# Head outputs of an mLSTM encoder turned by VectorE in 32x32 blocks instead of by TensorE, with the gates and the branch's DRAM copies laid out to match

## The chip, the cores and the metric

The kernel runs on one core of a Trainium2 chip. The metric is the device time of one execution in microseconds (us). The profile comes from one further execution, recorded by the hardware profiler.

## What is computed

One encoder layer over 1024 prompt tokens and 256 sample tokens with 1024 channels, all in float32. Cut to what matters here:

```python
h = rms_norm(x, norm_g) * (1.0 + scale) + shift          # scale, shift, gate from c @ w_ada
cb, cc, cx, cz, q, k, v, o, mz, gpre, gmerge = split(h @ w_in)
y_conv = cb * centred_dwconv3(cc * cx, conv_w, conv_b) * silu(cz)
h_fwd = mlstm_chunkwise(q, k, v, gates)                  # 4 heads of 256, chunks of 128 tokens
h_bwd = flip(mlstm_chunkwise(flip(q), flip(k), flip(v), flipped gates))
hm = h_fwd + h_bwd
hm = hm * rsqrt(mean(hm * hm, per head) + EPS) * mh_norm_g
y_m = sigmoid(o) * hm * silu(mz)
merged = sigmoid(g1) * (y_conv @ w_proj_conv) + sigmoid(g2) * (y_m @ w_proj_mlstm)
out = rms_norm(x + gate * (merged @ w_out), final_norm_g)
```

## The kernel before

Tokens of both sequences stand side by side, T = 1280, in ten chunks of 128 (eight and two). Large products are made of float32 operands split into a high and a low part (fp32r), three matmuls a product.

**Input projection** (to about 1180 us). Channels stand on partitions, tokens in the free dimension in two halves of 640. Strassen pairs (class Strassen; matmuls at L755, weight splits at L329 on ACT and L330 on POOL, evictions at L672) make in this order gate columns, head 0, og_pair, conv_pairs and the other heads. og_pair combines sigmoid(o) and silu(mz) into one gate (up to constant factors) and stores it by L797 and L802 as [channel, token] in og_dr, one DMA of 320 KB for a block of 128 channels and half of the tokens. by_tokens (L878) turns k and v by VectorE in blocks of 32x32 (L881) and stores each with four DMAs whose pieces are 32 floats long.

**Sweeps** (about 1180 to 1467 us). For each head one sweep over the chunks in one direction keeps its results in "kept", then a second one in the other direction runs while the next head's first does. Sweep.query (L1341) multiplies queries with the state C, Sweep.state (L1359) makes the state's update, which VectorE adds (L1365, L1367). Class Pairs finishes the second sweep two chunks at a time: scores (L1402), values (L1439 to L1460), and finish: RMS factor per token, scaled on ACT (L1482), then four transposes on TensorE (L1489) into two PSUM tiles "misc", a multiplication with the norm's weight mhq and the gate og on VectorE (L1492, reads PSUM, writes og), and two stores to ym_dr [channel, token] (L1499). Class Filler gives TensorE units of the convolution projection in between (L1581 to L1583); PACE says how many units are recorded by which step s.

**After the sweeps.** first_ym loads the second half of the tokens of ym_dr through the three "th" buffers, which the filler units use too, and splits it into high (L1602, ACT) and low (L1603, VectorE); it is called for heads 0 and 1 at step 45, for heads 2 and 3 behind the last step. merge runs the mLSTM projection (proj_y, L1514 to L1516; accumulators in eight PSUM banks that the sweeps' tiles held before), finish the output projection (L1726 to L1728). The first half's y is loaded by load_y (L1680 to L1682) meanwhile.

**What sets the order.** Up to the end of the sweeps the operations of all engines, SP's DMA issues among them, are recorded on a Board. It plays them as a list schedule by durations given by hand: what can start first goes first, within 0.25 us the lower step, and operations marked low last. Buffers of a tag go out in the order of their recording. All DMAs but a few small ones at the start are issued by SP, in that order, and each engine works through its queue in order. Behind the sweeps a scheduler orders the rest and may put its DMAs further ahead.

## Time and profile before

| | us |
|---|---|
| median of 3 runs (lowest, highest) | 1707.37 (1704.66, 1707.56) |
| the profiled execution | 1706.05 |
| its span, first to last instruction | 1704.3 |
| TensorE busy | 1657.9 (97%) |
| VectorE, ACT, POOL busy | 996.0, 579.4, 677.9 |
| DMA traffic | 241.87 MB, mean 142 GB/s |

Busy time counts any instruction on the engine. Matmuls are pipelined, so the distance between their starts, not their length, is what one costs. The granted clock was 0.993 on average. PE is TensorE, PEld its weight loads, DVE is VectorE, SPq the queue of SyncE that issues DMAs.

### The profile page before, as it was taken

Reading aid. Unit: us, or ns where it says so; the run is one execution under the profiler, and the core shown is the slowest. Engines: PE = TensorE matmul, PEld = TensorE weight load, DVE = VectorE, ACT = ScalarE, POOL = GpSimd, SP = SyncE. Lnnn points to the kernel's source line nnn. Section 1 sums busy time; section 2 is a strip of 40 time slices with the busy share of each in tenths; the row PEclk is TensorE's granted clock in tenths of the full one; section 3 lists DMA queues with packets and bytes.
Section 4 is the critical chain, followed back from the end, with each engine's and each line's share of the span. In section 5 each row is a group of like instructions: output and inputs, shape, how many; then the busy total and the mean of one; then the engine's idle time right before and its main releaser. Section 6 shows DMA issues by size and latency. Waiting matters only on the chain.

```text
span 1704.3 us, 27694 instructions
## 1 busy us (share of the span) xinstructions
PE 1657.9 (97%) x10542; PEld 1571.2 (92%) x10542; DVE 996.0 (58%) x1689; ACT 579.4 (34%) x1121; POOL 677.9 (40%) x499
## 2 busy tenths in 40 slices
PE   7889999999999999999999999999999999999997
PEld 1789999899999999999999999999988889898985
DVE  1795434456555655666666886652257777565645
ACT  2753232123544222222222222122256565333322
POOL 1124333234655576676667643333210101223412
PEclk9899999999999999999999999999999999999999
DMA  8224325323554122212222565558778855783631
GB/s 331 93 92 142 120 92 137 61 83 103 151 151 126 53 69 81 81 57 65 66 69 69 146 143 132 130 126 266 264 249 278 270 181 162 230 283 121 236 109 62
DMA packets 280536, 241.87 MB, mean 142 GB/s; under 512 B 96100, under 2 KB 237652, under 8 KB 280404
## 3 DMA queue, kind: packets, MB, share of 16 engines
q1 hardware_dynamic: 280224, 240.06, 46.1%
q8 instruction: 84, 1.38, 0.3%
q14 instruction: 48, 0.39, 0.1%
q10 hardware_dynamic: 180, 0.04, 0.0%
HBM read 171.16 MB, written 68.89 MB: 141 GB/s over the span
## 4 chain that ended last, share of the span: by engine, by line
PE 91%; DVE 4%; issue 1%; DMA 1%; ACT 1%; ACTq 0%; SPq 0%; POOL 0%; DVEq 0%; POOLq 0%
PE acc L755 61%; PE qc L1341 3%; PE u L1359 3%; PE accd L1515 2%; PE accd L1514 2%; PE accd L1516 2%; PE accd L1727 2%; PE accd L1728 2%; PE accd L1726 2%; PE acc L1582 2%; PE acc L1581 2%; PE acc L1583 2%; PE acc L480 2%; PE misc L1402 1%; PE misc L1442 1%
## 5 line engine op out<-in xcount | busy, mean ns | idle before, releaser
L330 POOL TENSOR_TENSOR wl<-comb,wh 128x512 fp32r<-128x512 f32 x176 | 248.2, 1411 | 290.2 <-ACT wh L329 277.8
L672 DVE TENSOR_TENSOR q<-acc,q 128x640 f32<-128x640 f32 x272 | 220.8, 819 | 217.5 <-PE acc L755 215.0
L330 POOL TENSOR_TENSOR wl<-raw,wh 128x512 fp32r<-128x512 f32 x136 | 190.0, 1398 | 243.8 <-ACT wh L329 240.7
L755 PE MATMUL acc<-xt,wh 128*128 128x320 f32 x1408 | 264.3, 310 | 0.0
L755 PEld LDWEIGHTS acc<-xt,wh 128*128 128x128 f32 x1408 | 220.8, 188 | 0.4
L329 ACT CAST wh<-comb 128x512 fp32r<-128x512 f32 x176 | 108.8, 619 | 285.4 <-PE acc L755 276.9
L329 ACT CAST wh<-raw 128x512 fp32r<-128x512 f32 x136 | 84.3, 621 | 281.9 <-PE acc L755 215.3
L755 PE MATMUL acc<-xt,wl 128*128 128x320 f32 x704 | 160.6, 310 | 0.0
L1542 POOL TENSOR_TENSOR wl<-raw,wh 128x512 fp32r<-128x512 f32 x28 | 36.3, 1299 | 232.2 <-ACT wh L1541 232.2
L755 PEld LDWEIGHTS acc<-xt,wl 128*128 128x128 f32 x704 | 117.7, 188 | 0.0
L628 DVE TENSOR_TENSOR comb<-raw 128x512 f32<-128x512 f32 x88 | 72.8, 827 | 47.3 <-DMA raw<-in_w_in_dram 31.0
L822 POOL TENSOR_TENSOR big<-big,q 128x640 f32<-128x640 f32 x48 | 78.6, 1638 | 36.9 <-DVE q L672 28.5
L572 ACT ACTIVATE q<-q,zero 128x640 f32<-128x640 f32 x76 | 63.2, 831 | 85.7 <-DVE q L672 78.6
L628 DVE TENSOR_TENSOR comb<-raw,comb 128x512 f32<-128x512 f32 x44 | 45.9, 1043 | 66.0 <-POOL wl L330 66.0
L755 PE MATMUL acc<-b11H,wh 128*128 128x320 f32 x352 | 81.4, 312 | 2.8 <-ACT wh L329 2.8
L755 PE MATMUL acc<-t2L,wh 128*128 128x320 f32 x352 | 80.2, 309 | 2.1 <-DVE t2L L384 2.1
L1514 PE MATMUL accd<-y,wh 128*128 128x320 f32 x256 | 79.6, 311 | 2.7 <-DVE og L1492 1.5
L755 PE MATMUL acc<-b00H,wh 128*128 128x320 f32 x352 | 81.9, 313 | 0.0
L755 PE MATMUL acc<-b10H,wh 128*128 128x320 f32 x352 | 80.7, 310 | 0.4 <-DVE q L672 0.4
L755 PE MATMUL acc<-t2H,wh 128*128 128x320 f32 x352 | 80.6, 310 | 0.4 <-ACT t2H L383 0.4
L755 PE MATMUL acc<-b11H,wl 128*128 128x320 f32 x352 | 80.5, 309 | 0.4 <-POOL wl L330 0.4
L755 PE MATMUL acc<-b11L,wh 128*128 128x320 f32 x352 | 80.6, 310 | 0.0
(318 smaller groups left out, 4151.1 us busy)
## 6 DMA issues: line engine op xcount, KB each, us to landing
raw<-in_w_in_dram SPq DMA_DIRECT2D x96, 256.0 KB
raw<-in_w_in_dram SPq DMA_DIRECT2D x46, 512.0 KB
th<-th_dr SPq DMA_DIRECT2D x32, 320.0 KB
th_dr<-q SPq DMA_DIRECT2D x28, 320.0 KB
raw<-in_w_proj_conv_dram SPq DMA_DIRECT2D x16, 512.0 KB
k<-kn_dr SPq DMA_DIRECT2D x64, 128.0 KB
raw<-in_w_proj_mlstm_dram SPq DMA_DIRECT2D x16, 512.0 KB
raw<-in_w_out_dram SPq DMA_DIRECT2D x16, 512.0 KB
```

Of the source, the lines that this page charges most:

```text
L329: op("ACT", .63, lambda: A.copy(wh[:], src()), r=r, w=[wh])
L330: op("POOL", 1.4, lambda: G.tensor_tensor(out=wl[:], in0=src(), in1=fp(wh[:]), op=ALU.subtract), r=[*r, wh], w=[wl])
L480: op("PE", .88, lambda h=h, j=j, kt=kt, wa=wa: PE.matmul(pada[h][0:4, j, :], cz4()[:, kt, :], wa()[:, j * 512:(j + 1) * 512], start=kt == ...
L572: A.activation(out, in_, AF.Tanh, bias=zero[:, 0:1], scale=0.5)
L628: op("DVE", .9, lambda: V.tensor_tensor(out=t[:], in0=x(), in1=y(), op=o), r=[x.tok, y.tok], w=[t])
L672: op("DVE", .82, lambda: V.tensor_tensor(out=two(dst()), in0=acc[:, :, 0:TQ], in1=two(t()), op=ALU.add), r=[acc, t.tok], w=[dst.tok])
L755: PE.matmul(acc[:, q, 0:TQ], st_[:, k_, :], m_[:, q * TQ:(q + 1) * TQ], start=k_ == 0 and n == 0, stop=k_ == 3 and n == 2)
L822: op("POOL", 1.65, lambda: G.tensor_tensor(out=dst(), in0=dst(), in1=t(), op=ALU.mult), r=[dst.tok, t.tok], w=[dst.tok])
L1341: PE.matmul(pq[:, 0:HD + 2], qTs[i][:, kd, c * P:(c + 1) * P], C[:, kd, :], start=kd == 0, stop=kd == 1)
L1359: PE.matmul(pu[:, db, 0:HD + 2], k[:, db * P:(db + 1) * P], wv[:], start=True, stop=True)
L1514: PE.matmul(accs[q][:, :TQ], wh, yH, start=kt == 0, stop=False)
L1542: op("POOL", 1.36, lambda wh=wh, wl=wl, src=src: G.tensor_tensor(out=wl[:], in0=src(), in1=fp(wh[:]), op=ALU.subtract), r=[raw, wh], w=[wl])
```

## The change

The head outputs of a pair are turned by one VectorE transpose, from SBUF to SBUF, in square blocks of 32x32 that stay in their place in the grid of blocks, and multiplied with the gate in a second VectorE operation. The gate is stored by og_pair in the matching order: og_dr is now [head, block of 32 tokens, channel in its block, block of channels, token in its block]; each of its 16 stores becomes four. The result goes to ym_dr, now [head, chunk, channel, token], by four DMAs for each pair in place of two, with pieces of 32 floats. The loads of ym_dr (first_ym, load_y) read it chunk by chunk, five pieces of 128 floats a channel in place of one of 640. The norm's weight mhq is left out of the sweeps' multiplication and applied where the loaded values are split: ACT's copy becomes a copy with scale, VectorE's subtraction a multiply and subtract. load_y does this a block of 128 channels at a time. Two more edits stand with it: PACE after step 21, and first_ym for heads 2 and 3 at step 50.

```diff
-    ym_dr = dram.tile([D, T], F32, name="ym_dr")
-    og_dr = dram.tile([D, T], F32, name="og_dr")
+    ym_dr = dram.tile([NH, NC, HD, P], F32, name="ym_dr")
+    og_dr = dram.tile([NH, T // 32, 32, HD // 32, 32], F32, name="og_dr")
...
+    def store_og(n, l, t):
+        for b in range(4):
+            store(80, og_dr[n // 2, l * 20:(l + 1) * 20, :, n % 2 * 4 + b, :].rearrange("x i j -> i x j"),
+                  lambda b=b: t()[32 * b:32 * b + 32].rearrange("p (x j) -> p x j", j=32), [t.tok])
...
-            store(320, og_dr[n * P:(n + 1) * P, lo_], to["o"], [to["o"].tok])
+            store_og(n, 0, to["o"])
...
-            store(320, og_dr[n * P:(n + 1) * P, hi_], t, [t.tok])
+            store_og(n, 1, t)
...
-            load(256, lambda: self.og[:], og_dr[h * HD:(h + 1) * HD, g * P:(g + 2) * P].rearrange("(b p) t -> p b t", p=P),
-                 (), [(self.og, 0), (self.og, 1)])
+            load(256, lambda: self.og[:], og_dr[h, 4 * g:4 * g + 8].rearrange("(c a) i b j -> (a i) c (b j)", a=4), (), [self.og])
...
-            for db in range(2):
-                py = buf(psB, [P, 512], F32, "misc", 3)
-
-                def turn(db=db, py=py):
-                    for j in range(2):
-                        PE.transpose(py[:, j * P:(j + 1) * P], qcf[:, j, db * P:(db + 1) * P], ident[:])
-
-                def gated(db=db, py=py):
-                    V.scalar_tensor_tensor(out=og[:, db, :], in0=py[:, :2 * P],
-                                           scalar=mhq[:, 2 * h + db:2 * h + db + 1], in1=og[:, db, :],
-                                           op0=ALU.mult, op1=ALU.mult)
-
-                r0 = h * HD + db * P
-                op("PE", .3, turn, r=[(qcf, 0), (qcf, 1)], w=[py])
-                op("DVE", .48, gated, r=[py, (og, db)], w=[(og, db)])
-                op("SP", 128, lambda db=db, r0=r0: dma(ym_dr[r0:r0 + P, g * P:(g + 2) * P], og[:, db, :]),
-                   r=[(og, db)], w=[("ym", h, g, db)])
+
+            z = buf(mp_, [P, 2, HD], F32, "z", 2)
+            op("DVE", .72, lambda: V.transpose(z[:], qcf[:, :, :HD]), r=[(qcf, 0), (qcf, 1)], w=[z])
+            op("DVE", .65, lambda: V.tensor_tensor(out=z[:], in0=z[:], in1=og[:], op=ALU.mult), r=[z, og], w=[z])
+            for a in range(4):
+                op("SP", 64, lambda a=a: dma(
+                    ym_dr[h, g:g + 2, :, 32 * a:32 * a + 32].rearrange("c (b i) j -> i (c b) j", i=32),
+                    z[32 * a:32 * a + 32].rearrange("p c (b j) -> p (c b) j", j=32)), r=[z], w=[("ym", h, g, a)])
...
+    def scaled_h(out, x, kt):
+        A.activation(out, x, AF.Copy, bias=0.0, scale=mhq[:, kt:kt + 1])
+
+    def scaled_l(out, x, hi, kt):
+        V.scalar_tensor_tensor(out=out, in0=x, scalar=mhq[:, kt:kt + 1], in1=fp(hi), op0=ALU.mult, op1=ALU.subtract)
...
-    PACE = [min(4 + s, 12) if s < 10 else 12 + (s - 9) * 4 // 7 if s < 17 else 16 if s < 21 else min(17 + (s - 21) * 13 // 28, 30) if s < 50 else 32
+    PACE = [min(4 + s, 12) if s < 10 else 12 + (s - 9) * 4 // 7 if s < 17 else 16 if s < 21 else min(16 + (s - 21) // 2, 32)
...
-        if s == 45:
-            ym0 = [first_ym(0)]
-    ym0.append(first_ym(1))
+        if s in (45, 50):
+            ym0.append(first_ym(s // 48))
...
-                dma(raw[:], v[:, 4 * n + k:4 * n + k + 2, t0:t0 + TH2])
-                A.copy(yH[:, k:k + 2], raw[:])
-                V.tensor_tensor(out=yL[:, k:k + 2], in0=raw[:], in1=fp(yH[:, k:k + 2]), op=ALU.subtract)
+                for j in range(2):
+                    dma(raw[:, j].rearrange("p (c t) -> p c t", t=P), ym_rows(4 * n + k + j, c0))
+                    scaled_h(yH[:, k + j], raw[:, j], 4 * n + k + j)
+                    scaled_l(yL[:, k + j], raw[:, j], yH[:, k + j], 4 * n + k + j)
```

## Rows read from the trace of the kernel before

**Rows 1.** The page: busy time of the engines; the chain that ended last.

```profile
PE 1657.9 (97%) x10542; PEld 1571.2 (92%) x10542; DVE 996.0 (58%) x1689; ACT 579.4 (34%) x1121; POOL 677.9 (40%) x499
...
PE 91%; DVE 4%; issue 1%; DMA 1%; ACT 1%; ACTq 0%; SPq 0%; POOL 0%; DVEq 0%; POOLq 0%
```

**Rows 2.** Stretches: busy us of PE, PEld, DVE, ACT, POOL; clock, DMA share, GB/s.

```profile
400.00:700.00 300.00, 300.00 (x2048) 300.00 (x2047) 175.47 (x183) 109.82 (x213) 180.28 (x125) 1.00 0.36 104
...
1265.00:1300.00 35.00, 34.44 (x192) 30.24 (x190) 24.54 (x84) 21.29 (x57) 3.81 (x3) 1.00 0.77 249
1300.00:1350.00 50.00, 48.93 (x276) 43.06 (x275) 37.50 (x132) 30.66 (x85) 2.56 (x2) 1.00 0.87 285
1350.00:1400.00 50.00, 50.00 (x283) 44.93 (x283) 37.89 (x135) 31.53 (x87) 3.82 (x3) 1.00 0.66 211
1400.00:1440.00 40.00, 39.55 (x245) 36.56 (x244) 31.52 (x114) 23.03 (x63) 6.49 (x5) 1.00 0.51 157
1440.00:1468.00 28.00, 26.21 (x174) 24.94 (x174) 19.65 (x59) 14.79 (x38) 8.17 (x6) 1.00 0.59 185
```

**Rows 3.** Timeline of PE, one pair's four turns: start us, us, what.

```profile
1435.41 0.60 PE L1489 MATMUL misc<-ident,qcf 128*128 128x128 f32 x4
1435.85 0.61 PE L1402 MATMUL misc<-kT,qT 128*128 128x128 f32 x4
```

**Rows 4.** Groups by line: shapes xcount | busy us, mean ns | idle before.

```profile
L1489 PE MATMUL misc<-ident,qcf 128*128 128x128 f32 x80 | 12.5, 275 | 0.3 <-ACT qcf L1482 0.2
...
L1492 DVE SCALAR_TENSOR_TENSOR og<-misc,mhq,og 128x256 f32<-128x256 f32 x40 | 17.5, 477 | 5.7 <-PE misc L1489 5.7
...
L881 DVE STREAM_TRANSPOSE q<-q 128x640 f32<-128x640 f32 x32 | 27.0, 845 | 1.1
```

**Rows 5.** Timeline of PE where the sweeps end.

```profile
1463.99 0.31 PE L1583 MATMUL acc<-b10H,wl 128*128 128x320 f32 x1
1464.48 0.95 PE L1489 MATMUL misc<-ident,qcf 128*128 128x128 f32 x4 [0.18 <-ACT qcf L1482]
1466.89 0.41 PE L1514 MATMUL accd<-y,wh 128*128 128x320 f32 x1 [1.46 <-DVE og L1492]
...
1470.52 0.31 PE L1514 MATMUL accd<-y,wh 128*128 128x320 f32 x1
1472.04 0.41 PE L1514 MATMUL accd<-y,wh 128*128 128x320 f32 x1 [1.20 <-ACT y L1602]
```

**Rows 6.** Timelines of DVE, SP and PE from there on.

```profile
1464.74 1.31 DVE L1603 TENSOR_TENSOR y<-th,y 128x640 fp32r<-128x640 f32 x1
1465.97 0.86 DVE L1492 SCALAR_TENSOR_TENSOR og<-misc,mhq,og 128x256 f32<-128x256 f32 x2
1466.42 0.38 SPq L318 DMA_DIRECT2D th<-ym_dr  x1
1472.02 0.83 DVE L1603 TENSOR_TENSOR y<-th,y 128x640 fp32r<-128x640 f32 x1 [3.38 <-ACT y L1602]
1549.71 1.49 DVE L1682 TENSOR_TENSOR y<-yraw,y 128x1280 fp32r<-128x1280 f32 x1 [1.76 <-ACT y L1681]
1575.84 0.40 PE L1728 MATMUL accd<-wh,mL 128*128 128x512 f32 x1
```

**Rows 7.** DMA issues by tile, ns min/median/max; then one stretch as in Rows 2.

```profile
L321 SPq DMA_DIRECT2D v_dr<-q x64: 302/508/1986, 303.3 to 1158.2; - x64
L321 SPq DMA_DIRECT2D og_dr<-q x16: 320/333/343, 386.3 to 560.6; - x16
L1499 SPq DMA_DIRECT2D ym_dr<-og x40: 319/378/1026, 1268.9 to 1467.4; - x40
...
1125.00:1126.00 1.00, 1.00 (x7) 0.94 (x7) 0.96 (x2) 0.01 (x1) 0.91 (x1) 1.00 0.97 144
```

**Rows 8.** Tile k: its loads and readers, ns min/median/max, first and last start.

```profile
L318 SPq DMA_DIRECT2D k<-kn_dr x64: 319/320/1750, 1182.4 to 1402.1; - x64
L1359 PE MATMUL u<-wv,k x256: 378/381/486, 1188.4 to 1430.5; 128*128 128x258 f32 x128
```

More of the change, by code (lines that the diff above doesn't have):

```diff
@@ L1592, in unit, with ym_rows @@
                 op("SP", 320, lambda: dma(zc_dr[n * P:(n + 1) * P, t0:t0 + TH2], th[:]), r=[(th, 0), (th, 1)], w=[("zc", n, b)])
+    def ym_rows(kt, c0):
+        return ym_dr[kt // 2, c0:c0 + 5, kt % 2 * P:(kt % 2 + 1) * P, :].rearrange("c p t -> p c t")
+    def scaled_h(out, x, kt):
+        A.activation(out, x, AF.Copy, bias=0.0, scale=mhq[:, kt:kt + 1])
+    def scaled_l(out, x, hi, kt):
+        V.scalar_tensor_tensor(out=out, in0=x, scalar=mhq[:, kt:kt + 1], in1=fp(hi), op0=ALU.mult, op1=ALU.subtract)
     def first_ym(n):
         y = [buf(yq, [P, 4, TH2], F32R, f"y{2 * n + part}", 1) for part in range(2)]
-        v = ym_dr[:].rearrange("(k p) t -> p k t", p=P)
         for k in range(4):
@@ L1600, in first_ym @@
             kt = 4 * n + k
-            load(320, lambda raw=raw, kt=kt: raw[:], v[:, kt, TH2:T], [("ym", kt // 2, g, kt % 2) for g in (4, 6, 8)], [raw])
-            op("ACT", .8, lambda raw=raw, k=k: A.copy(y[0][:, k], raw[:]), r=[raw], w=[(y[0], k)])
-            op("DVE", .9, lambda raw=raw, k=k: V.tensor_tensor(out=y[1][:, k], in0=raw[:], in1=fp(y[0][:, k]),
-                                                               op=ALU.subtract), r=[raw, (y[0], k)], w=[(y[1], k)])
+            load(320, lambda raw=raw: raw[:].rearrange("p (c t) -> p c t", t=P), ym_rows(kt, 5), [("ym", kt // 2, g, a) for g in (4, 6, 8) for a in range(4)], [raw])
+            op("ACT", .8, lambda raw=raw, k=k, kt=kt: scaled_h(y[0][:, k], raw[:], kt), r=[raw], w=[(y[0], k)])
+            op("DVE", .9, lambda raw=raw, k=k, kt=kt: scaled_l(y[1][:, k], raw[:], y[0][:, k], kt),
+               r=[raw, (y[0], k)], w=[(y[1], k)])
         return y
     fills = Filler()
-    PACE = [min(4 + s, 12) if s < 10 else 12 + (s - 9) * 4 // 7 if s < 17 else 16 if s < 21 else min(17 + (s - 21) * 13 // 28, 30) if s < 50 else 32
+    PACE = [min(4 + s, 12) if s < 10 else 12 + (s - 9) * 4 // 7 if s < 17 else 16 if s < 21 else min(16 + (s - 21) // 2, 32)
             for s in range(10 * NH + 15)]
     one, two_ = ([Sweep(h, (h < 2) ^ p, p) for h in range(NH)] for p in range(2))
-    prs = {}
+    prs, ym0 = {}, []
     def second(s):
@@ L1671, in encoder_kernel, with load_y @@
     yr = ctx.enter_context(tc.tile_pool(name="yr", bufs=1, side="right"))
-    def load_y(src, t0):
-        v = src[:].rearrange("(k p) t -> p k t", p=P)
+    def load_y(c0):
         res = []
@@ L1809, in encoder_kernel @@
         if ib:
-            y_m = load_y(ym_dr, HBS[0][0])
+            y_m = load_y(0)
         finish(5 * ib, ib == 0, mH, mL)
```

## The prediction

> **What bounds the kernel now.** I read the page's busy times and chain first, then one table by stretches, then the timeline where the sweeps end. The page shows TensorE busy 97% of the span and 91% of the chain on it [rows 1]: only work that leaves TensorE, or a gap on it that closes, can move the end by much. The table shows where there is room [rows 2]. Between 400 and 700 us (gates and convolution, Strassen products) TensorE is busy 300.00 of 300 us; nothing off it counts there while the product keeps being fed. From 1265 to 1468 us (the sweeps, while head outputs are finished and units of the convolution projection fill in) TensorE has 34.44, 48.93, 50.00, 39.55 and 26.21 us of 35, 50, 50, 40 and 28: 3.9 us without a matmul in 203. VectorE has 151 of the same 203 us, and the DMA engines' share is 0.77 and 0.87 in the first two stretches. So the sweeps are bound by TensorE's work, with VectorE and DMA next in line. The granted clock is 1.00 in all these stretches, the level of 2.4 GHz, so no term below has to do with the clock.
>
> **TensorE loses the turns (main term).** Line 1489 is 80 transposes, four for each of 20 pairs of chunks [rows 4]. The 275 ns that stand beside them are no price, since matmuls overlap; the price is from one start to the next. A group of four starts at 1435.41 and the scores that follow it at 1435.85 [rows 3]: 0.44 us, thus 20 x 0.44 = 8.8 us. What moves up is other TensorE work (sweep products, filler units), which is plentiful until the last steps, so I take all 8.8. Bounds: 5 if a part turns into gaps, 10 if the two PSUM buffers that each pair no longer asks for also end waits for "misc" tiles.
>
> **The seam after the sweeps.** At 1464.48 the last four turns start, and the first product of the mLSTM projection (L1514) not before 1466.89, after 1.46 us of idle time put down to og, L1492 [rows 5]. The projection's accumulators take over the PSUM of the sweeps, and the last reader of it is L1492, which at 1465.97 stands on VectorE behind a split of y (L1603) that began at 1464.74 [rows 6]. With the turn on VectorE, from SBUF to SBUF, the last PSUM readers are the combination with the values and the fillers' evictions, both earlier. From 1464.48 to 1466.89 are 2.41 us; less the 0.44 counted above, 1.97 us go. What is late next is y itself: the first accumulation stops again from 1470.52 to 1472.04 for its last part, loaded only at 1466.42 [rows 5, 6]; one product's step of 0.15 taken off, 1.37 us. The change records the loads of heads 2 and 3 at step 50, ahead of the last filler units, which shared the three "th" buffers with them; but they still need head 3's chunks 4 and 5 in DRAM, and TensorE will arrive earlier. I count half of it, 0.7 us, with ends of 1.4 gained and 1.5 lost.
>
> **VectorE gets more.** Out go 40 multiplications at 477 ns, 19.1 us [rows 4]. In come 20 transposes and 20 products of 128x512. The row nearest to the first is the 128x640 transpose, 845 ns, to scale 0.68 us [rows 4]. For the second there are 0.83 us at 640 elements and 1.49 at 1280 [rows 6], so about 0.70. Together 20 x 1.38 = 27.6 us, net +8.5 over 203 us: from 74% to some 82% in a stretch about 10 us shorter. I take its cost to the end at nothing, as TensorE nearly always has a second sweep or a filler to run while VectorE updates a state. If that cover were gone it is up to 8.5 us.
>
> **SP and the DMA engines get more.** Each pair stores with four DMAs of 512 pieces of 128 B where it had two of 256 KB in all with 1 KB pieces. Stores in the same small pieces exist in this trace, by_tokens, at 508 ns of SP each against 378 for today's ym store [rows 7]: 80 x 0.51 - 40 x 0.38 = 26 us more SP time. What is queued behind them on SP are the loads of k, of abc and og and of the heads to come. The k loads run ahead: the last is issued at 1402.1, the last product that reads one starts at 1430.5 [rows 8]; with six buffers and two sweeps the lead is about three steps. I take it at nothing; a delay below that lead costs nothing either. For the engines: while such stores ran alone, the share was 0.97 at 144 GB/s [rows 7], so a piece holds an engine for 0.97 x 16 x 128 / 144 = 13.8 ns, and a pair's 2048 pieces take 1.77 us of all sixteen. Today's 262 KB at the rate of 285 GB/s for a share of 0.87 [rows 2] take 0.80. Eight pairs fall between 1265 and 1350, +7.8 us, where the engines have 35 x 0.23 + 50 x 0.13 = 14.6 us free: it fits, with 7 us left, less some 3 that the faster stage uses up.
>
> DMA: Bandwidth & Descriptors (the Trainium skill, Specifications) puts the least size for line rate at 512 B and says that below it the engines read, modify and write. The trace agrees as far as the low 144 GB/s goes [rows 7]. If it meant a second pass not yet in that row, the rival below on the DMA engines would be the forecast.
>
> **Gates stored in blocks.** 16 stores of 320 KB become 64 of 80 KB in small pieces, 4 x 0.51 us of SP for 0.33 [rows 7], and each holds its q tile some 2 to 3 us longer. This lies between 386 and 561 us, where TensorE is busy all the time [rows 2]; head 0's and the other heads' by_tokens stores have the same form and more of them. Nothing, or up to 2 us if a q tile comes late at a pair. The loads of og keep 1 KB pieces.
>
> **The split with the norm's weight.** ACT copies with a scale in place of a plain copy, VectorE multiplies and subtracts in one pass: the same operands and length. For the second half load_y makes eight DMAs and eight smaller splits of four; its last split is at 1549.71, while TensorE still runs output products at 1575.84 [rows 6], so 25 us cover it. The new PACE hands out the units from step 21 to 53 at half a unit a step, one unit less at the end; the two that stood at step 50 come at 51 and 53, which helps the tail, where TensorE must wait for VectorE. Zero, with +-2 us for the order that is planned anew.
>
> **Sum.** 8.8 + 2.0 + 0.7 = 11.5 us off the profiled execution's 1706.05 gives 1694.6; the median of the runs is 1.3 above it, so 1695.9 for a median.
>
> **Rivals.** (a) VectorE's extra work shows. Its 8.5 us come out as gaps on TensorE: 1707.4 - 11.5 + 8.5 = 1704.4. For it: 38 busy us of 50 from 1300 to 1400 [rows 2], in order, and long operations that stand before a state update. Against it: TensorE has alternatives. Half of it gives 1700. (b) The DMA engines fill. If a small piece cost twice the row, eight pairs would add 8 x (3.54 - 0.80) = 21.9 us where about 12 are free, so some 10 us come back: 1706. At the row's own price there is no such loss; above about 20 ns a piece it begins. (c) Slower: every pair's transpose and product, 1.38 us, stand directly before the update of C on which both TensorE's next query and state wait, at moments when no filler is left. The price is up to 27.6 us, 1723; it decides from 0.58 us of new gap a pair (11.5 / 20). Against it: pairs finish four steps behind the sweeps, with filler units spread over all steps. (d) The turns go but the holes stay, because the recurrence and not the work sets the pace: 1707.4 - 2.7 = 1704.7. Against it: only 3.9 idle us in the stretch.
>
> **How the numbers follow.** Forecast 0.66 (1692 to 1699); a part of (a) or (b) 0.15 (1699 to 1704); (a), (b) or (d) in full 0.11 (about no change); (c) 0.07; a better seam and fewer PSUM waits, below 1690, 0.01. Measurements tell 0.2%, 3.4 us, from no change. Faster 0.82, same 0.11, slower 0.07. The range goes from 1690 (10 us by the turns, 3.4 by the seam, 4 of other gaps) to 1704.
>
> **What would show it.** Right: no L1489, TensorE without gaps up to L1514, the projection starting near 1456 us, VectorE near 82% from 1300 to 1400. The seam is right if L1514's first wait is shorter than 0.5 us. Wrong: TensorE's idle time before L1341 or L1359 put down to C (rival a or c); DMA shares at 1.0 with TensorE or ACT waiting for k or th (rival b); L755 idle between 386 and 561 us (the gates).

## The result and the profile after

The changed kernel takes 1713.12 us in the median (1710.47 to 1715.34), the kernel before beside it 1705.73 (1704.63 to 1707.56): ratio 1.0042, 95% interval 1.0027 to 1.0057. The change was to gain 11.5 us and it loses about 7. Its profiled execution took 1710.47 us with a span of 1708.7, 4.4 more than the span before, so the profile shows some 60% of the loss. Of the five executions the slowest has the lowest mean granted clock (0.988 at 1715.34 us, 0.990 in the profiled one), so time at 1.2 GHz is likely a part of the rest; no trace shows it.

First the engines' line of the page, then the stretches of [rows 2], now of the changed kernel (busy us of PE, PEld, DVE, ACT, POOL; clock, DMA share, GB/s):

```profile
PE 1650.5 (97%) x10462; PEld 1565.0 (92%) x10462; DVE 1009.2 (59%) x1693; ACT 581.4 (34%) x1125; POOL 679.0 (40%) x499
...
400.00:700.00 300.00, 298.41 (x2032) 297.68 (x2032) 175.52 (x183) 109.37 (x213) 180.27 (x124) 1.00 0.41 103
1265.00:1300.00 35.00, 31.74 (x173) 27.66 (x172) 26.14 (x84) 20.95 (x57) 3.82 (x3) 1.00 0.82 244
1300.00:1350.00 50.00, 46.41 (x242) 39.90 (x241) 38.94 (x135) 29.49 (x83) 1.27 (x1) 0.98 0.91 262
1350.00:1400.00 50.00, 49.99 (x271) 44.89 (x270) 41.64 (x138) 34.71 (x96) 3.83 (x3) 0.99 0.83 231
1440.00:1468.00 28.00, 23.33 (x153) 22.32 (x152) 22.14 (x56) 15.50 (x39) 8.25 (x6) 0.99 0.74 204
```

The 80 turns are gone (10542 matmuls became 10462). But TensorE now stands still where it did not: 1.6 us between 400 and 700, 6.9 instead of 1.6 between 1265 and 1350, and 4.7 instead of 1.8 between 1440 and 1468. The DMA share is up in every stretch of the sweeps.

The marks, as groups by line of the changed kernel (ns min/median/max, first and last start) and, last, one row of PE's timeline:

```profile
L1365 PE MATMUL u<-wv,k x256: 379/381/485, 1189.9 to 1434.0; 128*128 128x258 f32 x128
L1579 PE MATMUL acc<-b10H,wl x128: 305/308/468, 1182.9 to 1463.7; 128*128 128x320 f32 x128
L1491 DVE STREAM_TRANSPOSE z<-qcf x20: 699/706/714, 1264.7 to 1468.3; 128x512 f32<-128x512 f32 x20
L1492 DVE TENSOR_TENSOR z<-z,og x20: 673/692/694, 1265.5 to 1469.1; 128x512 f32<-128x512 f32 x20
L1494 SPq DMA_DIRECT2D ym_dr<-z x80: 313/488/1901, 1266.2 to 1471.2; - x80
...
1471.41 0.63 PE L1510 MATMUL accd<-y,wh 128*128 128x320 f32 x1 [7.38 <-DVE th L576]
```

The first state product starts 1.5 us later than before (1188.4, [rows 8]); the last one 3.5 later; the last filler product at 1463.7, 0.3 earlier [rows 5]; the first projection product 4.5 later. The gap ahead of it is 7.38 us where it was 1.46 [rows 5].

To compare kernels I use **uncovered time**: the length of a stretch, less, for each matmul that starts in it, the step at which matmuls of its kind follow one another at the full clock (0.147 us for 128x320, 0.218 for 128x258, 0.216 for 128x256, 0.109 for 128x128). From the profiled executions, one of each kernel, in us ("sweeps" from the first to the last state product, "seam" from the last filler product to the first projection product; "rest" is the whole time from that product to the end of the span):

| kernel | sweeps | seam | rest | ratio to before, interval |
|---|---|---|---|---|
| before | 10.3 | 2.3 | 237.4 | 1 |
| after | 16.6 | 7.5 | 237.3 | 1.0042, 1.0027 to 1.0057 |
| e1, last filler units early | 14.7 | 4.0 | 242.7 | 1.0033, 1.0020 to 1.0045 |
| e4, wide ym pieces | 13.4 | 4.9 | 238.7 | 1.0003, 0.9993 to 1.0013 |
| e6, all pieces wide | 13.4 | 5.0 | 237.5 | 0.9987, 0.9978 to 0.9996 |
| e3, before with the gates' blocks | 10.3 | 2.7 | 237.3 | 1.0016, 1.0008 to 1.0025 |
| e8, half of the exchange moved | 14.3 | 7.5 | 238.4 | 1.0019, 1.0010 to 1.0027 |
| e10, VectorE's transpose shrunk | 14.5 | 6.9 | 240.1 | 1.0029, 1.0017 to 1.0041 |
| e13, two casts off ACT | 15.2 | 5.4 | 237.1 | 1.0016, 1.0007 to 1.0026 |

**Where the sweeps lose.** Waits between 1265 and 1360 (us in total, times, longest), three of the changed kernel:

```profile
PE acc L1578 <- DMA b10L<-yc_drL: 2.0, 1, 2.0
PE u L1365 <- issue: 1.6, 1, 1.6
PE misc L1447 <- ACT Ps L1445: 1.2, 2, 0.8
```

None of the first kind stood in the kernel before. SP's queue just ahead of it (start us, us; xcount DMAs):

```profile
1335.09 3.10 SPq L1494 DMA_DIRECT2D ym_dr<-z  x4
1338.23 2.07 SPq L319 DMA_DIRECT2D og<-og_dr  x1
1340.40 1.81 SPq L319 DMA_DIRECT2D k<-kn_dr  x2
1342.26 0.43 SPq L319 DMA_DIRECT2D b10L<-yc_drL  x1
```

The four stores hold SP for 3.10 us, the next issues take 2.07 and 1.81 in place of the 0.3 to 0.5 that is usual. The last piece of the filler's operand y (b10L) goes out at 1342.26; TensorE wants it at 1345.2 and gets it at 1347.17. What follows on PE:

```profile
1347.17 0.41 PE L1578 MATMUL acc<-b10L,wh 128*128 128x320 f32 x1 [1.99 <-DMA b10L<-yc_drL]
...
1348.03 0.47 PE L1577 MATMUL acc<-b10H,wh 128*128 128x320 f32 x1
1348.29 0.47 PE L1578 MATMUL acc<-b10L,wh 128*128 128x320 f32 x1
...
1346.00:1348.00 2.00, 0.83 (x5) 0.83 (x6) 0.07 (x1) 0.75 (x3) 0.00 (x0) 1.00 1.06 374
1348.00:1350.00 2.00, 2.00 (x10) 2.00 (x9) 0.89 (x4) 0.36 (x1) 0.00 (x0) 0.50 1.02 192
```

From 1348 to 1351.4 the granted clock is 0.50, the level of 1.2 GHz: the products stand 0.27 us apart, not 0.15. Some 13 of them cost 13 x 0.12 = 1.6 us more. The 2 us wait thus costs 3.6.

**Where the gates lose.** Timelines of SP, POOL, ACT, VectorE and PE between 512 and 541:

```profile
512.19 5.78 SPq L322 DMA_DIRECT2D og_dr<-q  x8
520.78 0.37 SPq L319 DMA_DIRECT2D big<-a_dr  x1
...
529.58 1.28 POOL L1196 TENSOR_TENSOR big<-big,masks 128x512 f32<-128x512 f32 x1 [2.04 <-issue]
530.90 0.99 ACT L1200 ACTIVATE big<-big,gcol 128x128 f32<-128x128 f32 x3 [2.04 <-POOL big L1196]
533.16 1.34 DVE L576 SCALAR_TENSOR_TENSOR q<-q 128x640 f32<-128x640 f32 x1 [7.68 <-ACT q L573]
...
532.15 0.56 PE L756 MATMUL acc<-b00H,wl 128*128 128x320 f32 x2 [0.64 <-POOL wl L331]
540.06 0.53 PE L756 MATMUL acc<-t2H,wh 128*128 128x320 f32 x2 [0.92 <-DVE q L673]
```

Eight stores (two before, 3.50 us) keep SP busy for 5.78 us. The loads of the decay rows (a_dr) stand behind them, and POOL's mask addition (L1196) needs these rows. Behind the addition stand POOL's weight split (L331), for which TensorE waits 0.64 us, and ACT's work (L1200, then L573), for which VectorE waits 7.68 us; so VectorE's next eviction (L673) is late, and TensorE waits 0.92 us for it. The profile names no releaser for POOL's wait of 2.04 us. In the kernel before the same addition waits for the load, less long, and TensorE has no gap there:

```profile
527.21 1.29 POOL L1190 TENSOR_TENSOR big<-big,masks 128x512 f32<-128x512 f32 x1 [1.54 <-DMA big<-a_dr]
```

The addition comes 2.4 us later now, 0.8 of it because all of that stretch stands 0.8 later.

**Where the seam loses.** ACT, VectorE and the clock, from the last filler's end on:

```profile
1462.21 0.62 ACT L288 CAST wh<-raw 128x512 fp32r<-128x512 f32 x1 [2.73 <-PE acc L1578]
...
1463.59 1.28 DVE L1598 SCALAR_TENSOR_TENSOR y<-th,mhq,y 128x640 fp32r<-128x640 f32 x1 [2.41 <-ACT y L1595]
1469.07 0.69 DVE L1492 TENSOR_TENSOR z<-z,og 128x512 f32<-128x512 f32 x1
1470.47 0.88 DVE L576 SCALAR_TENSOR_TENSOR th<-th,acc 128x320 f32<-128x320 f32 x2
...
1468.00:1471.00 3.00, 0.00 (x0) 0.00 (x0) 2.79 (x6) 1.00 (x2) 0.00 (x0) 0.50 0.10 16
1471.00:1480.00 9.00, 8.59 (x50) 8.60 (x50) 0.84 (x2) 0.62 (x1) 1.13 (x1) 0.82 0.88 230
```

The last PSUM readers are the two last evictions of filler results, L576, at 1470.47, at the very end of VectorE's queue: behind the splits of y and behind the whole head norm, turn and product of the last pair. That chain in turn starts late, since ACT's cast of a projection weight (L288) waited 2.73 us for a weight buffer that the last fillers held. The last of these evictions stood well ahead of the last pair's multiplication (1465.97, [rows 6]) in the kernel before:

```profile
1464.33 0.49 DVE L575 SCALAR_TENSOR_TENSOR th<-th,acc 128x320 f32<-128x320 f32 x1 [0.82 <-PE acc L1583]
```

The projection then starts at the clock of 1.2 GHz.

### The profile page after: what moved, and what is told of

It reads as the page before. It is cut to its first block, busy times and chain, and to the rows that moved or that the text cites. A ratio compares the mean times of both kernels' runs of the same rounds, so it can differ in the third digit from the quotient of the medians.

```text
span 1708.7 us, 27697 instructions
## 1 busy us (share of the span) xinstructions
PE 1650.5 (97%) x10462; PEld 1565.0 (92%) x10462; DVE 1009.2 (59%) x1693; ACT 581.4 (34%) x1125; POOL 679.0 (40%) x499
## 5 line engine op out<-in xcount | busy, mean ns | idle before, releaser
L331 POOL TENSOR_TENSOR wl<-comb,wh 128x512 fp32r<-128x512 f32 x176 | 248.1, 1410 | 287.4 <-ACT wh L330 275.1
L673 DVE TENSOR_TENSOR q<-acc,q 128x640 f32<-128x640 f32 x272 | 220.8, 819 | 209.1 <-PE acc L756 203.8
L331 POOL TENSOR_TENSOR wl<-raw,wh 128x512 fp32r<-128x512 f32 x136 | 191.3, 1407 | 241.0 <-ACT wh L330 237.8
L573 ACT ACTIVATE q<-q,zero 128x640 f32<-128x640 f32 x76 | 63.1, 831 | 85.3 <-DVE q L673 76.7
L576 DVE SCALAR_TENSOR_TENSOR q<-q 128x640 f32<-128x640 f32 x48 | 56.8, 1183 | 42.4 <-ACT q L573 42.2
L756 PE MATMUL acc<-b00H,wl 128*128 128x320 f32 x352 | 80.4, 309 | 0.6 <-POOL wl L331 0.6
```

Of the source, the lines that this page charges most:

```text
L331: op("POOL", 1.4, lambda: G.tensor_tensor(out=wl[:], in0=src(), in1=fp(wh[:]), op=ALU.subtract), r=[*r, wh], w=[wl])
L573: A.activation(out, in_, AF.Tanh, bias=zero[:, 0:1], scale=0.5)
L576: V.scalar_tensor_tensor(out=out, in0=th, scalar=1.0, in1=x, op0=ALU.add, op1=ALU.mult)
L673: op("DVE", .82, lambda: V.tensor_tensor(out=two(dst()), in0=acc[:, :, 0:TQ], in1=two(t()), op=ALU.add), r=[acc, t.tok], w=[dst.tok])
L756: PE.matmul(acc[:, q, 0:TQ], st_[:, k_, :], m_[:, q * TQ:(q + 1) * TQ], start=k_ == 0 and n == 0, stop=k_ == 3 and n == 2)
```

## The experiments

Four groups, each with the share it was to measure. A difference between kernels is taken from the ratios, times 1706 us; the interval of such a difference is some 2 to 3 us to either side.

**The pieces of 128 bytes in the sweeps (e4, e8).** e4 stores the same 80 DMAs with rows of 2 KB, so values stand in other places:

```diff
-  ym_dr[h, g:g + 2, :, 32 * a:32 * a + 32].rearrange("c (b i) j -> i (c b) j", i=32), z[32 * a:32 * a + 32] in blocks of 32
+  ym_dr[h, g:g + 2] as 128 rows of 2 KB, rows [32 * a:32 * a + 32], z[32 * a:32 * a + 32] whole
```

> The changed kernel with the same 80 stores of head outputs, but each writes 32 rows of 2 KB in the order in which they stand, not 512 pieces of 128 B; the values land in the wrong places, so the output differs from the reference. Theory D (the DMA engines): the pieces raise the DMA share from 0.87 to 0.91 between 1300 and 1350 us and make k and y come late; without them the share falls below 0.87 and TensorE's gaps from 1265 to 1350 (8.6 us at present, 3 in the kernel before) fall by 4 to 5 us: 1708 to 1709. Rival V (VectorE's longer operations): the gaps stay, 1712 to 1714.

Measured: 1706.23 (1702.35 to 1709.99), ratio 1.0003. That is 0.0039 or 6.7 us less than the changed kernel, 3.5 us by the spans of the two profiled executions. In the profile the wait for b10L is gone; the first of the two slices above reads

```profile
1346.00:1348.00 2.00, 2.00 (x17) 2.00 (x16) 1.90 (x11) 0.89 (x4) 0.00 (x0) 1.00 0.89 283
```

and the other two waits of the list stand there unchanged (1.6 and 1.2 us). The wait for b10L is in all seven traces that have every small piece and TensorE's order of the changed kernel in the sweeps (1.1 to 2.4 us; the changed kernel, e1, e2, e7, e10, e13, e14) and not in e4, e6, e8 or e15. So the 3.2 us in the sweeps are the pieces'. Two things go with them: the engines' load and SP's time, for in e4 the four stores ahead of b10L hold SP for 1.72 us, not 3.10, and the load goes out at 1340.57, not 1342.26. No run parts the two.

The 2.6 us at the seam are not the pieces' alone. The scheduler of what stands behind the sweeps has put ACT's casts of projection weights elsewhere in e4 (and in e6), behind the last pair's square sums, where they wait for nothing:

```profile
1460.64 0.60 ACT L288 CAST wh<-raw 128x512 fp32r<-128x512 f32 x1
1466.51 0.64 PE L1510 MATMUL accd<-y,wh 128*128 128x320 f32 x1 [4.73 <-DVE th L576]
```

e13, below, moves only these casts and has nearly the same seam. Nor is all of it gain: after the first projection product the clock stays at 1.2 GHz for 6.0 us in e4 and 2.9 in the changed kernel, and half of that is lost; the table's "rest" is 1.4 longer. The DMA table for 1265 to 1440 (packets; then packets, MB, share of 16 engines) gives the price of a piece. After:

```profile
DMA packets 63160, 39.63 MB, mean 226 GB/s; under 512 B 37840, under 2 KB 56487, under 8 KB 63143
q1 hardware_dynamic: 63143, 39.42, 80.2%
```

and e4:

```profile
DMA packets 32831, 41.06 MB, mean 235 GB/s; under 512 B 3104, under 2 KB 23885, under 8 KB 32813
q1 hardware_dynamic: 32813, 40.85, 74.4%
```

34,736 more small pieces take 5.8% of 175 us more, 10.2 us of all 16 engines, though 1.4 MB less was moved, which at the rate of 285 GB/s for a share of 0.87 [rows 2] is another 4.4. So 14.6 x 16 / 34,736 = 6.7 ns a piece on top of the 6.2 that its bytes take at that rate: some 12.9 ns of packet time, twice the wide price.

e8 computes the whole layer: pairs of chunks 0 to 3 (8 of 20) store z in 1 KB rows, one DMA each, and load_y exchanges the blocks during the projection:

```diff
+  if g < 4: dma(yz_dr[h, g:g + 2] as [token block and channel, chunk, block and token], z[:])
+  # load_y: for b in range(4): 32 rows of raw <- yz_dr[kt // 2, :, :, x0:x0 + 32] in pieces of 32 floats
```

> The changed kernel with the same result, in which the pairs of chunks 0 to 3 (8 of the 20) store their product in rows of 1 KB, one DMA instead of four, and the exchange of blocks of that half is made where it is loaded, behind the sweeps (40 loads instead of 8 during the first half of the projection). 40 per cent of the small pieces leave the sweeps. Theory 'small pieces in the sweeps cost 7 us, in proportion': 2.8 us less, 1709.5 to 1710.5, ratio 1.002 to 1.003, provided the later loads are hidden. Theory 'only the pieces around the seam cost': 1712 to 1713. Rival: the 40 loads of the first half come late or hold up SP's weight loads, and the projection shows waits of over 3 us for y or the weights: 1713 or more.

Measured: 1709.72 (1706.67 to 1712.73), ratio 1.0019: 3.9 us less than after, where 40% of the pieces would be 2.7 of e4's 6.7. In the sweeps the wait for b10L is gone. ACT's casts stand as in the changed kernel, and the seam is as long, 7.5. The 40 loads show no wait on TensorE: its "rest" is 1.1 longer, but so is the time at 1.2 GHz after the first projection product (5.6 us, not 2.9).

**The gates' pieces (e3, e6, e11).** e3 is the kernel before with only the gate's block layout, stores and loads:

```diff
-  og_dr = dram.tile([D, T], F32, name="og_dr")
+  og_dr = dram.tile([NH, T // 32, 32, HD // 32, 32], F32, name="og_dr")     # stored by store_og, loaded by blocks
```

> The kernel before with the gates' part alone: stored with their blocks exchanged in 64 stores of small pieces, and loaded in that layout; the head outputs are still turned by TensorE, so they meet gates in the wrong place and the output differs from the reference. Theory G: the added stores delay the loads for the decay weights on SP, POOL waits for those in order and splits a weight late: TensorE loses about 2 us between 500 and 560 us, 1707 to 1709 against 1705.7. Rival: hidden, within 1 us of before.

Measured: 1709.41 (1706.38 to 1710.29), ratio 1.0016, 2.7 us slower (1.4 to 4.3). Its trace shows one gap of TensorE for it, 1.00 us before the product at 539.24, the one that waits for VectorE's eviction; the wait for POOL's split is not there. e6 is e4 with the gates stored in rows as well (and loaded from them):

```diff
-  store(80, og_dr[n // 2, l * 20:(l + 1) * 20, :, n % 2 * 4 + b, :] in pieces of 32 floats, ...)
+  store(80, og_dr[n * P + 32 * b:n * P + 32 * b + 32, l * TH2:(l + 1) * TH2], ...)
```

> The changed kernel with the sweeps' stores and the gates' stores both in rows of full length (2 KB and 5 KB), the same number of DMAs; neither the blocks of the outputs nor those of the gates are exchanged, so the values of the mLSTM branch stand in other places. Theory 'the pieces of 128 bytes cost twice, 7 us at the sweeps and 3 us at the gates, and the turns save what was forecast less the seam': 1702.5 to 1704, ratio 0.997 to 0.999. Theory 'the gates' cost comes from the count of their DMAs on SP, not from the size of the pieces': 1706, ratio 1.000, as with the sweeps' stores alone. Theory 'the two do not add': 1706.

Measured: 1703.68 (1702.28 to 1708.45), ratio 0.9987, 2.7 us less than e4 (0.4 to 5), with the same number of DMAs. TensorE's stretch is nearly whole again:

```profile
400.00:700.00 300.00, 299.80 (x2045) 299.57 (x2044) 176.82 (x184) 109.81 (x214) 183.38 (x126) 1.00 0.38 103
```

So it is the size of the pieces, twice measured at 2.7 us; the gaps that the traces show for it are 1.0 to 1.6. And even without any exchange the change is worth 2.2 us (0.7 to 3.8), not 11.5. e11 tried to get the gates' share back by marking their stores low, on top of e8 and a fourth th buffer:

```diff
-  store(80, og_dr[...], ..., [t.tok])
+  op("SP", 80, lambda b=b: dma(og_dr[...], ...), r=[t.tok], low=True)
```

> Same result as the changed kernel: exchange of the first half behind the sweeps (measured: 3.4 us less), a fourth buffer th, and the gates' stores placed behind the weight loads on SP where both could go. Theory 'the shares add': 3.4 from the exchange, 1 to 3 from the seam, 1 to 2 of the gates' 3 us: 1705 to 1707, ratio 0.999 to 1.000. Rival 'a gain ahead of the seam is eaten by the seam, whose last link is VectorE's chain': 1709 to 1710. Rival 'the gates' cost is their pieces on the DMA engines, not their place on SP': 1706.5 to 1708.

Measured: 1735.40 (1735.15 to 1737.16), ratio 1.0174. The stores go out later, the last at 583.0 instead of 563.1, and TensorE then waits for evictions into q tiles (waits between 380 and 600), as if the stores kept these tiles until they are issued:

```profile
PE acc L757 <- DVE q L674: 14.7, 6, 4.9
```

That was expected by neither theory nor rival. Their place on SP cannot simply be given to the loads.

**VectorE (e5, e10).** e5 leaves the block transpose out, the product reads the combination:

```diff
-  op("DVE", .72, lambda: V.transpose(z[:], qcf[:, :, :HD]), ...)
-  V.tensor_tensor(out=z[:], in0=z[:], in1=og[:], op=ALU.mult)
+  V.tensor_tensor(out=z[:], in0=qcf[:, :, :HD], in1=og[:], op=ALU.mult)
```

> The changed kernel without VectorE's block transpose: the product with the gate reads the combination directly, so the channels and tokens of the mLSTM branch are not turned and the output is another one; stores, loads and gates are as changed. VectorE loses 20 x 0.70 = 14 us, 9.8 of them in 1265 to 1440. Theory 'small pieces only': TensorE's uncovered time from 1265 to the last state product stays at 12 to 13 us (13.1 in the changed kernel), the time at 1711 to 1713. Theory 'VectorE's added work holds TensorE' (the part that wide pieces left, 9.8 against 6.4 before): uncovered time 9 to 10, time 1708 to 1709.5, ratio to the kernel before 1.0015 or less. If only the latency of one more operation at the seam counts: the time moves 0.7 us.

Measured: 1709.15 (1704.42 to 1711.31), ratio 1.0007. By its time it would speak for VectorE's added work, but it mixes two things: with 0.7 us less on the list the planner put 24 more filler products ahead of the last state product, the sweeps show 21.0 us uncovered and the seam 2.9. e10 keeps TensorE's order in the sweeps as it was and shrinks the operation:

```diff
-  V.transpose(z[:], qcf[:, :, :HD])
+  V.transpose(z[:, 0, :32], qcf[:, 0, :32])      # the product then reads qcf; the planned cost stays .72
```

> The changed kernel with VectorE's block transpose cut from 128x512 to 128x32 at the same place in every queue (the order of TensorE, ACT and SP in the sweeps is the same; leaving it out altogether had moved filler units, so that test mixed two things). The outputs of the sweeps are not turned. VectorE loses about 0.55 x 20 = 11 us. Theory 'VectorE's added work is part of what TensorE waits for': uncovered time from 1265 to the last state product 9 to 11 us instead of 13.1 and 1 us less at the seam: time 1708.5 to 1710, ratio 1.001 to 1.002. Theory 'only the pieces': the time stays at 1711.5 to 1713, ratio 1.003 to 1.004.

Measured: 1711.76 (1708.33 to 1712.77), ratio 1.0029; the interval overlaps that of the changed kernel. In the profile the sweeps go from 16.6 to 14.5 us, but that is the wait for b10L and its clock again. The wait is shorter and the clock does not fall after it (the wait; then the stretch, against 0.98 above):

```profile
PE acc L1578 <- DMA b10L<-yc_drL: 1.5, 1, 1.5
...
1300.00:1350.00 50.00, 46.88 (x250) 40.04 (x249) 37.63 (x139) 30.16 (x84) 1.53 (x2) 1.00 0.91 263
```

Less that, both have the same left: 16.6 - 2.0 - 1.6 = 13.0 and 14.5 - 1.5 = 13.0. So in the profiles VectorE's block turn holds nothing inside the sweeps, and 0.6 us at the seam. By the ratios e10 is 2.2 us faster than the changed kernel, and anything from none to some 5 us fits.

**The seam (e1, e2, e7, e9, e12 to e15).** e1 puts the last two filler units at step 50 as before; e2 records first_ym for heads 2 and 3 behind the last step, as before:

```diff
-  else min(16 + (s - 21) // 2, 32)                        # e1
+  else 16 + (s - 21) // 2 if s < 50 else 32
-  if s in (45, 50): ym0.append(first_ym(s // 48))         # e2
+  if s == 45: ym0.append(first_ym(0))   ...   ym0.append(first_ym(1)) behind the loop
```

> The changed kernel with one edit: the last two filler units are recorded at step 50 again, ahead of the y loads of heads 2 and 3. Theory S (the seam): in the changed kernel TensorE stands idle 7.7 us before the projection because the last units' evictions wait for gate tiles whose buffers come behind four y loads. Then the idle time before the projection falls to 3 us or less, the granted clock does not fall there, and the time is 5 to 7 us below the changed kernel's 1713, about 1707. Rival (the tail's own chain): the gap comes from the last pair's operations on VectorE and stays at 6 us or more, put down to another line; time within 2 us of 1713.

> The changed kernel with one edit: the y loads of heads 2 and 3 recorded behind the last step, as before; the new pace of units stays. Theory S: the idle time before the projection falls as in e1 (to 3 us or less), while the wait for the last part of y inside the first accumulation comes back (1 to 3 us): about 1708. Rival: no change against 1713.

Measured: e1 1711.38 (1707.85 to 1713.36), ratio 1.0033, seam 4.0; e2 1710.22 (1707.71 to 1715.04), ratio 1.0026, seam 5.6. Neither interval is clear of the changed kernel's. In e1 the last two evictions stand ahead of the last pair's turn (1467.41) on VectorE, and the first projection product comes at 1466.89, as in the kernel before:

```profile
1463.89 0.47 DVE L576 SCALAR_TENSOR_TENSOR th<-th,acc 128x320 f32<-128x320 f32 x1
1466.35 0.48 DVE L576 SCALAR_TENSOR_TENSOR th<-th,acc 128x320 f32<-128x320 f32 x1
```

So it is the new PACE that put them behind that turn. But what e1 gains at the seam it loses again: its "rest" is 5.4 us longer, with waits for weights of the projection (1.24 us on PE at 1488.65 and 0.89 behind it) and the clock at 1.2 GHz for 5.9 us after the first projection product and for 3.4 more at these waits. Neither edit, taken back alone, gives the loss back.

e7 takes the last pair's way through DRAM away: the last head's rows of y are loaded from the head before.

```diff
-  load(320, ..., ym_rows(kt, 5), [("ym", kt // 2, g, a) ...], [raw])
+  load(320, ..., ym_rows(min(kt, 5), 5), [("ym", min(kt, 5) // 2, g, a) ...], [raw])
```

> The changed kernel in which the last head's half of y (rows 768 to 1023 of the second half) is loaded from the rows of the head before, so that part of the mLSTM branch is computed from other rows; nothing at the end of the sweeps waits any more for the last pair's way through DRAM. All DMAs, splits and gates stay. Theory 'the last pair's round trip and what stands behind it on SP and VectorE make the seam late': first projection at 1465 to 1467 instead of 1471.4, uncovered time of the seam 2 to 4 us instead of 7.5, no fall of the clock there, time 1708 to 1709.5, ratio 1.001 to 1.002. Theory 'the seam only takes up what would be waited for later (weights of the projection)': first projection early, but the time stays at 1711 to 1713. By bounds from the seam edits made so far (2 to 3 us) about 1710.

Measured: 1710.86 (1708.65 to 1713.99), ratio 1.0026, and the first projection product, 8.1 us after the last filler product:

```profile
1472.48 0.63 PE L1510 MATMUL accd<-y,wh 128*128 128x320 f32 x1 [7.76 <-DVE th L576]
```

My theory of the round trip fell: the projection does not wait for it, and the seam is as long (7.9). e9 gives the tiles th a fourth buffer, e12 does so in the kernel before:

```diff
-  buf(thp, [P, TH2], F32, "th", 3)
+  buf(thp, [P, TH2], F32, "th", 4)
```

> The changed kernel with four buffers instead of three for the tiles th, which the fillers' gates and the raw rows of y share at the end of the sweeps; nothing else. Taking the last round trip away left the seam at 7.9 us of uncovered time, so what holds there must be something else: in the changed kernel the last two evictions (L576) stand on VectorE behind the split of y and behind the last pair's head norm, and the last filler's gate is loaded only when a split has given a th buffer back. Theory 'buffers of th': with a fourth the gate is loaded before the y rows, the evictions come earlier, uncovered time of the seam 2 to 4 us instead of 7.5, time 1709 to 1710.5. Theory 'the order on VectorE and ACT (weight split waiting for the filler's buffers ahead of the last norm)': the seam stays at 6 to 8 us, time 1711 to 1713.

> The kernel before with a fourth buffer th, the control for the two kernels that have one: if that buffer is worth something by itself, it is so here too. Its seam shows 2.3 us uncovered, so at most 2 us can come: 1704.5 to 1706.5, ratio 0.999 to 1.000 by every theory; a larger gain would mean that the seam of both kernels hangs on these buffers.

Measured: e9 1716.46 (1715.27 to 1718.79), ratio 1.0063; e12 1708.86 (1707.37 to 1710.40), ratio 1.0017. The seams are shorter, 4.3 and 1.1 us, but the plan of the first steps is another one and more is lost there, against every expectation. Both spent 10.0 and 9.2 us uncovered before 1265, against 3.5 and 3.9. In e12 TensorE waits there for a head's queries, whose load went out behind other loads (3.8 us the same wait in e9), and the clock falls in that wait and stays at 1.2 GHz to 1251.6:

```profile
1247.08 2.09 PE L1341 MATMUL qc<-C,qT 128*128 128x258 f32 x4 [4.56 <-DMA qT<-qT_dr]
```

e13 has the two casts of the first projection's second weight block made by POOL; e14 leaves them and moves the low splits of y of heads 2 and 3 to POOL (they leave the norm's weight out there).

```diff
-  A.copy(wh[:], src)                                      # e13, split_w, for that block alone
+  eng.tensor_copy(wh[:], src)
-  op("DVE", .9, lambda ...: scaled_l(y[1][:, k], ...), ...)        # e14, n == 1
+  op("POOL", 1.8, lambda ...: G.tensor_tensor(out=y[1][:, k], in0=raw[:], in1=fp(y[0][:, k]), op=ALU.subtract), ...)
```

> The changed kernel with the high halves of the first projection's second weight block (two of the casts L288, those that stand in ACT's queue between the last pairs' work and wait there for the last filler to give its weight buffers back) made by POOL instead; same result. Theory 'ACT stands 2.7 us at that cast, and the last pair's norm, the y split and through VectorE the last evictions stand behind it': first projection 2 to 3 us after where it was earlier, about 1468.5 to 1469.5, seam 4.5 to 5.5 us uncovered instead of 7.5, time 2 to 3 us less, 1709.5 to 1711, ratio 1.002 to 1.003. Theory 'the y split's place on VectorE ahead of the evictions': seam 6.5 to 7.5, time 1711.5 to 1713.

> The changed kernel with the four low splits of the second half of first_ym made by POOL instead of VectorE (they leave the head norm's weight out of the low half, so that part of the output is another one); TensorE's order in the sweeps is the same. Theory 'VectorE's y splits (0.88 and 1.28 us each, three of them between the last filler and the first projection, one waiting 2.4 us) hold the evictions': the evictions come right behind the last filler or its gate's load, seam 3 to 5 us uncovered instead of 7.5, time 1709 to 1711. Theory 'ACT's weight split ahead of the last norm': the evictions still stand behind the last norm, seam 6 to 7.5, time 1711 to 1713. If the gate's load (th buffer given back by POOL, later) decides instead: seam 7.5 or more.

Measured: e13 1708.79 (1707.63 to 1712.94), ratio 1.0016, 4.4 us less than after by the ratios, of which the profile shows 2.1 at the seam and 1.4 in the sweeps (which the edit does not reach: b10L is waited for 1.55 us there, and the clock does not fall after it); e14 1711.41 (1709.90 to 1714.14), ratio 1.0032. First the end of the filler and the seam in e13, whose evictions are L579:

```profile
1463.66 0.31 PE L1586 MATMUL acc<-b10H,wl 128*128 128x320 f32 x1
1469.25 0.63 PE L1517 MATMUL accd<-y,wh 128*128 128x320 f32 x1 [5.28 <-DVE th L579]
```

then e14:

```profile
1461.67 0.62 ACT L288 CAST wh<-raw 128x512 fp32r<-128x512 f32 x1 [2.88 <-PE acc L1578]
1464.58 0.59 DVE L1473 TENSOR_SCALAR ssqm<-ssqm 128x2 f32<-128x2 f32 x1 [4.09 <-ACT junk L1465]
1471.54 0.64 PE L1510 MATMUL accd<-y,wh 128*128 128x320 f32 x1 [8.06 <-DVE th L576]
```

Without the casts ACT does not stand, and the projection starts 5.6 us after the last filler product, not 7.7; the orders of TensorE and VectorE are the changed kernel's. Without the splits of y on VectorE the seam is no shorter: VectorE waits 4.09 us for the last pair's square sums, which stand on ACT behind the cast. So the cast is the cause of about 2.1 us of the seam. The rest, some 3 us over the kernel before, is by the timelines the last pair's own chain ahead of the evictions in VectorE's queue, as e1 shows from the other side; no run takes that chain alone away. e15 is e8 with the edit of e13:

> Same result as the changed kernel: exchange of the first half behind the sweeps (3.4 us less by itself) together with the two casts made by POOL. If the shares add as the theory of ACT's cast says: 1706.5 to 1708, ratio 1.000 to 1.001; if the cast is not what holds: 1709 to 1710.5, as the half exchange alone.

Measured: 1708.77 (1706.70 to 1709.52), ratio 1.0013, only 1.0 us below e8, with intervals that overlap: the seam is 5.1 instead of 7.5, but the shares add only in part. None of the versions that compute the whole layer is faster than the kernel before. Doing only the 8 pairs of e8 on VectorE would, by estimate, save 8 x 0.44 = 3.5 us of turns and cost 0.4 x 2.7 = 1.1 at the gates and some of the seam, which is hardly more than these runs can tell from nothing; no run shows it.

## Why the prediction was wrong, by its steps

**What bounds the kernel.** Right: TensorE does, and every loss that the traces show is a gap on TensorE or a slower clock after one. That "no term below has to do with the clock" was wrong: it fell in or behind the new gaps.

**The turns, 8.8 us.** Nothing contradicts it, but no run isolates it. Uncovered time rises by 6.3 in the sweeps, 5.2 at the seam and 0.8 beside them, and the Strassen products end 1.0 later (1178.4 to 1179.4); 13.3 - 8.8 = 4.5, against 4.4 of span. That is bookkeeping and no test of the 8.8, since uncovered time itself counts each turn at its step of 0.109 us (80 x 0.109 = 8.7).

**The seam, 2.7 us to be gained: the first step that failed.** "The last PSUM readers are the combination with the values and the fillers' evictions, both earlier". The evictions are the last readers and came later, not earlier: at 1470.47, not 1464.33. They stand in VectorE's order behind the last pair's norm, turn and product, where the new PACE put them (e1). With less TensorE work the fillers end at the same time but the chain of the last pair (ACT, VectorE, ACT, VectorE) is as long as ever, and the cast on ACT made it start late (2.1 us, e13). I had followed which instruction reads PSUM, not what is queued ahead of it on its engine. The part on y was half right: the second wait in the projection (1.37 us, [rows 5]) is gone; the slow clock took its place (ten products at 0.27 us, 10 x 0.12 = 1.2).

**VectorE, 0 us.** Right in size (0.706 and 0.692 us for the 0.68 and 0.70 worked out; 80.6 busy us of the 100 from 1300 to 1400, where 82% was the sign). For its cost e10's profile speaks: nothing in the sweeps, 0.6 us at the seam; the ratios of e10 leave room for up to 5 us.

**SP and the DMA engines, 0 us: the second step that failed.** The price of a piece was right, 12.9 ns against 13.8, and SP's 488 ns against 508. Wrong was "it fits, with 7 us left": I compared sums over 85 us. From 1300 to 1350 the engines' share went from 0.87 to 0.91 on average, but a load that goes out last, behind four stores, where the share is 1.06 and 1.02, is late all the same; and it was a load that the step did not list (it named k, abc, og and the heads; the fillers' own y, b10L, stands in the same queue). By the profiles this costs 3.2 us in the sweeps, the wait and the slow clock after it. e4's 6.7 us also hold a part of the seam that goes with ACT's other order. Rival (b) named this mechanism and then ruled it out "at the row's own price"; it happens at that price. DMA: Bandwidth & Descriptors (the Trainium skill, Specifications) puts the least size for line rate at 512 B; the traces agree, with a factor of two for pieces of 128 B, 12.9 against 6.2 ns.

**The gates, 0 to 2 us: the third.** Twice measured at 2.7, with intervals that reach into the range. The step looked at TensorE's busy row and at q tiles. What was late was a load behind the stores on SP, then POOL, then a weight split on it and, through ACT, an eviction of VectorE's.

**Split and PACE, 0 +- 2.** Taking the edits back changes the time by 1.5 and 2.7 us (e1, e2), not told apart from nothing. That the new PACE "helps the tail" was wrong: it put the last evictions behind the last pair (e1).

**What the sum missed as a whole.** By the ratios: of the 8.8 us of turns 2.2 are left when no piece is small (e6). Most of the other 6.6 stands in e6's profile as gaps that wide pieces leave too: 5.0 - 2.3 = 2.7 at the seam and 13.4 - 10.3 = 3.1 in the sweeps. The small pieces, sweeps and gates together, then turn 2.2 us gained into 7.2 lost: 9.4 us, give or take 3, ACT's other order in e6 included. For the 3.1 in the sweeps the cause stays open. Waits that are new there (for Ps of ACT, and 1.6 us ahead of L1365 that the profile puts to no releaser) stand in e4 and nearly so in e10 alike, so neither pieces nor, by the profile, VectorE's transpose makes them; that the order was planned anew is likely, but was not shown.

VectorE: DVE Perf Modes (the Trainium skill, The three transpose paths and Rules for kernel authors) recommends TensorE for a 128x128 transpose where PSUM can take it, and says that VectorE turns only blocks of 32x32. This case agrees, with a number: exchanging the blocks that are left over by DMA pieces cost about as much, 9.4 us, as the whole turn had cost on TensorE, 8.8.

## What to carry to other kernels

Work taken off the bounding engine is worth what the next queue can deliver: before counting it, list every load that is issued behind the new stores on the in-order DMA queue and look at the one with the least lead, in the fullest slice, not at the mean share of a long stretch. Where a pool of PSUM is handed over, follow the last reader's whole queue (VectorE and ACT), since an instruction that is early in dataflow may be last in order; and see whether the time gained there is not waited for right behind it (e1). A block transpose that leaves the exchange of blocks to DMA trades one cheap matmul for many small pieces, at twice the price of their bytes.

## What the hardware showed

A wait of 2.0 us on TensorE, which from 1335 on had been busy 9.12 of the 10.18 us before it, was followed by 3.4 us at the 1.2 GHz level: it cost 3.6 us, not 2.0. At the same place the clock also fell after waits of 1.9 (e14) and 2.4 us (e7), and did not after 1.1 to 1.6 (e1, e2, e10, e13). The length alone does not tell: at the first state product a wait of 1.9 us (e2) was followed by 3.4 us at 1.2 GHz, one of 2.3 us (e6) was not. At the seam the clock fell within gaps of 3.79 (e1), 4.73 (e4), 5.28 (e13) and 7.38 us, and not within the 1.46 us of the kernel before. A gap of 2 us or more is to be counted with what it may do to the clock after it.
